# Decoder trunk on one core: forms of x tile by tile, its norm after the first gated steps, early gated tiles and weights, x tiles at multiples of 512 bytes

## The chip, the core and the metric

The kernel runs on one core of a Trainium2 chip. TensorE (PE) multiplies, VectorE (DVE) and ScalarE (ACT) prepare operands and empty PSUM, GpSimd (POOL) adds and issues accumulating DMAs, SyncE (SP) issues all other DMAs. The metric is the device time of one execution in microseconds, as the median of several runs.

## The reference

One decoder layer on 512 tokens with width 2048, in float32:

```python
h = rmsnorm(x, attn_norm)
aq, ak, av, bq, bk, bv, cq, ck, cv = split(h @ w_in)
mix = concat(rmsnorm(window_attention(aq, ak, av)), rmsnorm(stick_breaking(bq, bk, bv)),
             rmsnorm(dilated_attention(cq, ck, cv)))
x = x + mix @ w_out
h = rmsnorm(x, ffn_norm)
u = causal_dwconv(h @ w_up, conv_w, conv_b)      # width 3; w_up is 2048 x 11264
gate, up = split(u)
x = x + (silu(gate) * up) @ w_down               # w_down is 5632 x 2048
```

## The kernel before

Everything is held transposed, as tiles of 128 features by 512 tokens. A float32 product is made of three matmuls of rounded parts (`mm3`): high by high, high by low, low by high. Weights come through the three buffers `wr` in 512 KB pieces (list `stream`, `load_next`); `split` makes the parts `wh` (ACT copy) and `wl` (DVE subtraction) of each half.

The program has four stages on PE.

1. The input projection and attention. The normalised input stands in 32 tiles `x` (high and low of 16 k-tiles) of the pool `xp`, the first pool from the right end of the memory. These tiles are the moving operand of 2400 matmuls of 512 columns, with attention matmuls between them. As the built program places them, each `x` tile begins 480 bytes past a multiple of 512; the other tiles that long runs of matmuls read (`mc`, `th`, `tl`, `g`) begin at multiples of 512, because the pool `tp` has a tile `end` of 480 bytes at its right end.
2. The second half of the output projection: 16 products of 24 matmuls that read the tiles `mc`. Each result goes through `projected(m)` (line 963): DVE multiplies by the row norm `rg` and adds the first half, reloaded from `xab_dram` into one of three buffers `xn`; ACT scales it to `xb`; SP stores it to `xm_dram` and reloads `xn` for m + 3 into the buffer that this store reads; for every second m, `forms` makes the seven sums of halves of two tiles, rounded into `TH` and the remainders into `TL`; `sumsq` squares on ACT (`tq`) and adds on POOL into `gacc`. Behind the last tile `row_rstd` multiplies a matrix of ones by `gacc` on PE (tile `c`), and a short chain on ACT, POOL and DVE gives the rows `r2` and `nr2`.
3. The up-projection: 44 units u of seven steps (a11, p, q, a12, v, r, a22), s = 7u + j; each step is 24 matmuls of 256 columns with `TH` and `TL`. `cast(s + 3)` on ACT and `rest(s + 3)` on DVE make a step's weight parts `hi` and `lo`, three steps ahead. The weights p and v are sums of two blocks: SP loads one, POOL issues a DMA that adds the other. q and r are sums made on DVE (`add_raw`). `after(s)` takes results out of PSUM, applies r2, the convolution and the gate, and stores the gated tile to `g_dram`.
4. The down-projection: gated tiles are reloaded (`gates`: load, ACT copy, DVE subtraction) and multiplied by `w_down`, six sums at a time in chunks of eight tiles, then ten further products.

Between stages 2 and 3, and 3 and 4, `clock.drain()` issues everything that is queued, the `c` product among it, before the next stage's matmuls. The order on each engine is written at build time: tasks wait on a modelled clock (`Clock`) and their instructions are placed when that clock reaches them; on the chip each engine's queue then runs in that order, and an instruction that waits holds up all behind it. SP's queue too.

## Time and profile before

| what | us |
|---|---|
| median of 3 runs (lowest, highest) | 2207.19 (2206.53, 2208.12) |
| the profiled execution, its own time | 2207.63 |
| its span, first to last instruction | 2205.8 |
| PE busy in the span | 2163.0 (98%) |
| DVE busy, ACT busy | 1453.4 (66%), 1148.5 (52%) |
| stage 2, starts of the first and last matmul that read `mc` | 709.18, 799.75 |
| stage 3, starts of its first and last matmul | 817.73, 1706.37 |

The page's busy time of PE counts overlapping matmuls, so it is not PE at its peak; the distance from one matmul's start to the next is read from the timeline or from long runs in the chain of waits. Waits are read by stage.

### The profile page before, as it was taken

The page shows a single profiled execution, that of the slowest core. Times are in us where ns is not written, and L with a number is a line of the kernel's source. Part 1 is how long each engine was busy: PE and PEld are TensorE (multiplying, and loading weights), DVE is VectorE, ACT ScalarE, POOL GpSimd, SP SyncE. Part 2 cuts the span into 40 slices and gives each one's busy share as a digit, 9 for nine tenths or more (in the row PEclk, how much of TensorE's full clock was granted, in tenths as well). Part 3 has the DMA queues.
Part 4 walks back from the last instruction along what each step waited for, and adds up shares of the span by engine and source line. Part 5 has one row for each costly group of instructions (what it writes and reads, how often), then busy time and mean ns, then how long its engine had stood idle before and what let it go on. Part 6 is the DMA issues. An engine that isn't in the chain of part 4 may idle for free.

```text
span 2205.8 us, 34567 instructions
## 1 busy us (share of the span) xinstructions
PE 2163.0 (98%) x13236; PEld 1935.8 (88%) x13236; DVE 1453.4 (66%) x2229; ACT 1148.5 (52%) x2020; POOL 181.5 (8%) x241
## 2 busy tenths in 40 slices
PE   8999999999999969999999999999999899999999
PEld 6888888888888859999999999999999688888887
DVE  7677777767755687888888888788877434322222
ACT  6778667776663555555555555555554333222221
POOL 4000100110000120000000000000000000000000
PEclk9999999999999989999999999999999899999999
DMA  6322343334657557777777777777773554433332
GB/s 199 99 91 82 105 143 126 109 122 131 211 181 236 160 163 199 189 200 188 204 194 196 195 197 192 200 200 196 193 198 107 201 168 143 158 115 115 116 123 73
DMA packets 124013, 353.82 MB, mean 160 GB/s; under 512 B 14328, under 2 KB 17784, under 8 KB 123848
## 3 DMA queue, kind: packets, MB, share of 16 engines
q1 hardware_dynamic: 111176, 305.47, 41.7%
q0 software_dynamic: 12672, 46.14, 12.9%
q8 instruction: 104, 1.70, 0.3%
q14 instruction: 61, 0.50, 0.1%
HBM read 312.18 MB, written 32.57 MB: 156 GB/s over the span
## 4 chain that ended last, share of the span: by engine, by line
PE 94%; DMA 3%; DVE 1%; issue 1%; ACT 0%; SPq 0%; POOL 0%; DVEq 0%; POOLq 0%; ACTq 0%
PE s L51 50%; PE pj L51 39%; PE po L51 3%; PE c L51 2%; DMA xm_dram<-xn 1%; DMA wr<-in_w_out_dram 1%; DVE wl L51 0%; DVE tl L51 0%; DMA xn<-xab_dram 0%; DMA wr<-in_w_in_dram 0%; SPq L129 0%; DMA g<-g_dram 0%; DMA wr<-in_w_up_dram 0%; DMA st<-in_xT_dram 0%; POOL gacc L51 0%
## 5 line engine op out<-in xcount | busy, mean ns | idle before, releaser
L51 PE MATMUL s<-th,hi 128*128 128x256 f32 x2464 | 698.6, 284 | 0.0
L51 PE MATMUL s<-tl,hi 128*128 128x256 f32 x2464 | 697.7, 283 | 0.0
L51 PE MATMUL s<-th,lo 128*128 128x256 f32 x2464 | 697.7, 283 | 0.0
L51 DVE TENSOR_TENSOR wl<-wr,wh 128x512 fp32r<-128x512 f32 (+2 forms) x430 | 298.0, 698 | 342.2 <-ACT wh L51 340.5
L51 ACT CAST wh<-wr 128x512 fp32r<-128x512 f32 (+2 forms) x430 | 256.3, 598 | 486.4 <-PE pj L51 310.0
L51 PE MATMUL pj<-x,wh 128*128 128x512 f32 x1504 | 479.2, 400 | 0.0
L51 PEld LDWEIGHTS s<-th,hi 128*128 128x128 f32 x2464 | 473.6, 192 | 0.5 <-issue 0.5
L51 PEld LDWEIGHTS s<-tl,hi 128*128 128x128 f32 x2464 | 473.6, 192 | 0.5 <-issue 0.5
L51 PEld LDWEIGHTS s<-th,lo 128*128 128x128 f32 x2464 | 473.5, 192 | 0.0
L51 PEld LDWEIGHTS pj<-x,wh 128*128 128x128 f32 x1504 | 271.4, 188 | 55.7 <-issue 2.7
L51 PE MATMUL pj<-x,wl 128*128 128x512 f32 x752 | 297.1, 395 | 0.0
L51 PE MATMUL pj<-g,wh 128*128 128x512 f32 x880 | 271.0, 389 | 0.0
L51 PEld LDWEIGHTS pj<-g,wh 128*128 128x128 f32 x880 | 165.2, 188 | 34.5
L51 DVE TENSOR_TENSOR lo<-sm,hi 128x1024 fp32r<-128x1024 f32 x88 | 107.9, 1226 | 103.8 <-ACT hi L51 103.8
L51 PE MATMUL pj<-g,wl 128*128 128x512 f32 x440 | 171.2, 389 | 0.0
L51 PEld LDWEIGHTS pj<-x,wl 128*128 128x128 f32 x752 | 141.2, 188 | 33.9
L51 ACT CAST hi<-sm 128x1024 fp32r<-128x1024 f32 x88 | 92.3, 1049 | 139.7 <-DVE sm L51 139.7
L51 DVE TENSOR_TENSOR lo<-ld,hi 128x1024 fp32r<-128x1024 f32 x111 | 137.0, 1234 | 28.9 <-ACT hi L51 28.9
L51 DVE TENSOR_TENSOR lo<-wr,hi 128x1024 fp32r<-128x1024 f32 x109 | 133.1, 1221 | 28.2 <-ACT hi L51 28.2
L51 ACT CAST hi<-ld 128x1024 fp32r<-128x1024 f32 x111 | 116.5, 1050 | 21.7 <-PE s L51 21.7
L51 ACT CAST hi<-wr 128x1024 fp32r<-128x1024 f32 x109 | 114.4, 1050 | 22.2 <-PE s L51 20.7
L51 PE MATMUL s<-g,wh 128*128 128x512 f32 x352 | 110.7, 396 | 13.5 <-ACT g L51 13.3
(168 smaller groups left out, 2716.6 us busy)
## 6 DMA issues: line engine op xcount, KB each, us to landing
ld<-in_w_up_dram SPq DMA_DIRECT2D x111, 512.0 KB, 4.5
wr<-in_w_up_dram SPq DMA_DIRECT2D x109, 512.0 KB, 4.6
wr<-in_w_down_dram SPq DMA_DIRECT2D x80, 512.0 KB, 3.5
wr<-in_w_in_dram SPq DMA_DIRECT2D x78, 512.0 KB, 3.6
ld<-in_w_up_dram POOLq DMA_DIRECT2D x45, 512.0 KB, 5.6
wr<-in_w_up_dram POOLq DMA_DIRECT2D x43, 512.0 KB, 5.6
wr<-in_w_out_dram SPq DMA_DIRECT2D x32, 512.0 KB, 4.3
g_dram<-wl SPq DMA_DIRECT2D x44, 256.0 KB, 2.6
```

The source lines that it names most:

```text
L51: res = issue(out, *args, **kwargs)
```

## The change

Stage 1: a new first pool `ep` at the right end holds the 480 byte tile `end`, so that `xp` and its `x` tiles begin at multiples of 512. Nothing else moves there: but for that one memset, the instructions of every engine keep their order up to the end of this stage.

Stage 2 to 3: `forms` becomes `even_forms`, run for the even tile of a pair (the forms 0 and 3), and `odd_forms` for the odd one. `xn` has four buffers, `xb` three. The weights of steps 0 and 1 come as two more pieces of `stream`, split in halves like `w_out`; q of the first unit is summed early. There is no drain: the 48 matmuls of steps 0 and 1 follow the last product directly, step 2 is placed when the last odd forms are, the `c` product comes between the steps 3 and 4, and r2 is wanted in `after(6)`.

Stage 3 to 4: the gated tiles 0 to 4 are brought in during unit 41 into buffers of `xn`, `xb` and `tq`; the first three pieces of `w_down` are fetched and split as if they were steps of a unit 44; the first three sums run over tiles 0 to 4 at once, then over 5 to 7, with the last `after` steps between. There is no drain here either.

```diff
+        ep = ctx.enter_context(tc.tile_pool(name="ep", bufs=1, side="right"))
...
+        stream += ["a11", "p"]
...
+                if isinstance(stream[i], str):
+                    arrival = fetch(0, stream[i])
+                    raws[i] = got[0, stream[i]], arrival
+                else:
+                    piece = wp.tile([128, stream[i].shape[1]], F32, name="wr", bufs=3)
+                    raws[i] = piece, load(piece, stream[i])
...
+        vector.memset(ep.tile([128, 120], F32, name="end"), 0.0)
...
+                    ready["xab", m] = True
...
+        tx = ctx.enter_context(tc.tile_pool(name="tx", bufs=1, side="right", reuse_waits="tile"))
         tp = tctx.enter_context(tc.tile_pool(name="tp", bufs=1, side="right", reuse_waits="tile"))
         tr = tctx.enter_context(tc.tile_pool(name="tr", bufs=1, side="right", reuse_waits="tile"))
+        cv = tx.tile([128, SM_N - SM_CONV + 32], F32, name="conv")
...
-        vector.memset(tp.tile([128, 120], F32, name="end"), 0.0)
...
-            t = tr.tile([128, S], F32, name="xn", bufs=3)
+            t = tx.tile([128, S], F32, name="xn", bufs=4)
...
+        def low(j, t, a, b):
+            vector.tensor_sub(TL[j][:, a * HS:b * HS], t, TH[j][:, a * HS:b * HS].bitcast(F32))
+        def even_forms(j):
+            a = xb[2 * j]
+            while j > 1 and ("odd", j - 2) not in ready:
+                yield 0.1
+            f = quarters[j] = tr.tile([128, 4 * HS], F32, name="sm", bufs=2)
+            scalar.copy(TH[j][:, :HS], a[:, :HS])
+            vector.tensor_sub(f[:, :HS], a[:, :HS], a[:, HS:])
+            yield
+            scalar.copy(TH[j][:, 3 * HS:4 * HS], f[:, :HS])
+            low(j, a[:, :HS], 0, 1)
+            yield
+            low(j, f[:, :HS], 3, 4)
+            ready["even", j] = True
+        def odd_forms(j):
...
+            vector.scalar_tensor_tensor(q[2], b[:, HS:], -1.0, q[0], op0=ALU.mult, op1=ALU.subtract)
+            yield
+            scalar.copy(TH[j][:, 5 * HS:6 * HS], q[2])
+            scalar.copy(TH[j][:, HS:3 * HS], b)
             vector.tensor_sub(q[1], b[:, HS:], a[:, HS:])
-            scalar.copy(TH[j][:, HS:3 * HS], b)
-            vector.scalar_tensor_tensor(q[2], b[:, HS:], -1.0, q[0], op0=ALU.mult, op1=ALU.subtract)
             vector.scalar_tensor_tensor(q[3], q[2], -1.0, b[:, :HS], op0=ALU.mult, op1=ALU.subtract)
+            low(j, q[2], 5, 6)
...
+            scalar.copy(TH[j][:, 4 * HS:5 * HS], q[1])
+            scalar.copy(TH[j][:, 6 * HS:], q[3])
+            low(j, b, 1, 3)
...
+            low(j, q[1], 4, 5)
+            low(j, q[3], 6, 7)
+            ready["odd", j] = True
...
+                yield from (odd_forms if m % 2 else even_forms)(m // 2)
...
+            if u == NFF:
+                return load(t, w_down[0][DOWN.index(name)])
...
+                first = u == 0 and name == "q"
+                t = got[u, name] = place() if first else tr.tile([128, 1024], F32, name="sm", bufs=2)
+                vector.tensor_add(t, got[u, a], got[u, b])
...
+        def first_sum():
+            while len(raws) < len(stream):
+                yield 0.1
+            yield max(raws[len(stream) - 1][1] - clock.now(), 0.01)
+            fetch(0, "a12")
+            add_raw(0, "q", "p", "a11")
...
-            fetch(0, "v")
-            fetch(0, "a22")
-            for x in range(3):
-                if x == 2:
-                    add_raw(0, "q", "p", "a11")
-                cast(x)
-                yield
-                rest(x)
-                yield
-        spawn(ahead())
-        clock.drain()
...
+        while (0, "q") not in got:
+            idle()
+        def second():
+            cast(2)
+            yield
+            rest(2)
+        spawn(second())
+        fetch(0, "v")
+        fetch(0, "a22")
...
+            if s == 2:
+                add_raw(u, "r", "q", "a12")
...
-        for j in range(5):
-            after(7 * NFF + j)
-        clock.drain()
...
-        GS = {f: [gq.tile([128, S], F32R, name=f"g{x}_{f}") for x in range(2)]
-              for f in [*range(36, NFF), *range(36)]}
...
+            while s == 2 and ("odd", 7) not in ready or s == 6 and "r2" not in ready:
+                idle()
+            after(s)
+            if u == NFF - 3 and j < 5:
+                names = [f"tq{i}" if i < 3 else "xb" if i < 6 else "xn" for i in (2 * j, 2 * j + 1)]
+                GS[j] = [tx.tile([128, S], F32R, name=x, bufs={"xn": 4, "xb": 3}.get(x, 1)) for x in names]
+                spawn(gates(j))
...
+            pieces = operands(s)
+            per = 8 // len(pieces)
+            for k in range(8):
+                while ("even" if form in (0, 3) else "odd", k) not in ready:
+                    idle()
+                hi, lo = pieces[k // per]
...
-        for x in range(3):
-            split_next()
...
-        sums = [ps.tile([128, S], F32, name=x, bufs=1) for x in ("s0", "s1", "s2", "s3", "po0", "c0")]
-        for f in range(8):
-            spawn(gates(f))
+        sums = [ps.tile([128, S], F32, name=x, bufs=1) for x in ("s0", "s2", "po0", "c0", "s1", "s3")]
+        for f in range(5, NFF - 8):
+            GS[f] = [gq.tile([128, S], F32R, name=f"g{x}_{f}") for x in range(2)]
+            if f < 8:
+                spawn(gates(f))
...
+        def first_part(m, ks):
+            hi, lo = ops[7 * NFF + m][0]
+            for k in ks:
+                while ("g", k) not in ready:
+                    idle()
+                mm3(sums[m], hi, lo, k, ready["g", k], k == 0, False)
+                clock.run()
+        for m in range(3):
+            first_part(m, range(5))
+            after(7 * NFF + m)
+            clock.run()
+        for m in range(3):
+            first_part(m, range(5, 8))
+            if m < 2:
+                after(7 * NFF + 3 + m)
+            clock.run()
+            if m == 1:
+                for x in range(3):
+                    split_next()
+        for i, f in enumerate(range(NFF - 8, NFF)):
+            t = wq.tile([128, 1024], F32R, name="hi" if i < 4 else "lo", bufs=4)
+            GS[f] = [t[:, :S], t[:, S:]]
```

PE at the end of stage 2. Before, from the last row of the output projection; `c` is the product for the norm, `th` and `tl` the forms, `hi` and `lo` weight parts:

```order
L51 MATMUL pj0_8158<-mc_7278,wl_8121 128x512
L51 MATMUL c0_8247<-gacc_83,cst_78 128x512
L51 MATMUL s0_8258<-th0_7394,hi_8211 128x256
L51 MATMUL s0_8258<-tl0_7402,hi_8211 128x256
L51 MATMUL s0_8258<-th0_7394,lo_8212 128x256
```

And now, the same place:

```order
L51 MATMUL pj0_8211<-mc_7283,wl_8161 128x512
L51 MATMUL s0_8262<-th0_7404,wh_8181 128x256
L51 MATMUL s0_8262<-tl0_7412,wh_8181 128x256
L51 MATMUL s0_8262<-th0_7404,wl_8182 128x256
L51 MATMUL s0_8262<-th1_7405,wh_8181 128x256
```

The `c` product has gone from between the two stages; it stands 96 matmuls later.

DVE at the same place, now, from the multiplication that takes the last product out of PSUM (`tq2<-pj0`; `wl_8280` is the low part of p's second half, `lo_8277` that of q, `lo_8270` that of a12, `tl7` the remainders of the last pair):

```order
L51 TENSOR_TENSOR tq2_8250<-pj0_8211,r1_83 128x512
L51 TENSOR_TENSOR xn_8141<-tq2_8250,xn_8141 128x512
L51 TENSOR_TENSOR lo_8270<-ld_8201,hi_8269 128x1024
L51 TENSOR_TENSOR sm_8150<-xb_8195,xb_8138 128x256
L51 SCALAR_TENSOR_TENSOR sm_8150<-sm_8150,xb_8195 128x256
L51 TENSOR_TENSOR tl6_7418<-sm_8150,th6_7410 128x256
L51 TENSOR_TENSOR sm_8290<-xb_8247 128x256
L51 TENSOR_TENSOR lo_8277<-wr_8203,hi_8276 128x1024
L51 TENSOR_TENSOR wl_8280<-ld_8117,wh_8279 128x512
L51 TENSOR_TENSOR tl6_7418<-xb_8195,th6_7410 128x512
L51 TENSOR_TENSOR tl7_7419<-xb_8247,th7_7411 128x256
```

The remainder that step 0 reads last stands eleventh in that row, behind parts of q, p and a12; before, all of `tl7` was written before DVE read `c`.

POOL, before, with the three last additions for the norm behind the accumulating DMA of v:

```order
L51 TENSOR_TENSOR gacc_83<-gacc_83,tq2_8150 128x512
L1007 DMA wr_8206<-in_w_up_dram 128x1024
L51 TENSOR_TENSOR gacc_83<-gacc_83,tq1_8185 128x512
L51 TENSOR_TENSOR gacc_83<-gacc_83,tq0_8215 128x512
L51 TENSOR_TENSOR gacc_83<-gacc_83,tq1_8238 128x512
```

And now, with two DMAs ahead of them, v of unit 0 (`wr`) and p of unit 1 (`ld`):

```order
L51 TENSOR_TENSOR gacc_86<-gacc_86,tq0_8206 128x512
L1044 DMA wr_8257<-in_w_up_dram 128x1024
L1044 DMA ld_8266<-in_w_up_dram 128x1024
L51 TENSOR_TENSOR gacc_86<-gacc_86,tq1_8317 128x512
L51 TENSOR_TENSOR gacc_86<-gacc_86,tq0_8323 128x512
L51 TENSOR_TENSOR gacc_86<-gacc_86,tq2_8371 128x512
```

The additions now stand behind a second transfer as well.

## Rows read from the trace of the kernel before

**Rows 1.** The page: span, busy time of PE, and its clock in 40 slices.

```profile
span 2205.8 us, 34567 instructions
PE 2163.0 (98%) x13236; PEld 1935.8 (88%) x13236; DVE 1453.4 (66%) x2229; ACT 1148.5 (52%) x2020; POOL 181.5 (8%) x241
PEclk9999999999999989999999999999999899999999
```

**Rows 2.** Waits of PE: who waited for whom, us in total, times, longest.

```profile
PE c L51 <- POOL gacc L51: 16.5, 1, 16.5
PE s L51 <- ACT g L51: 13.3, 1, 13.3
```

**Rows 3.** The chain of waits, long runs of matmuls: start, us, what, count.

```profile
46.11 11.89 PE pj L51 x51
...
818.71 887.95 PE s L51 x7392
...
1902.86 299.21 PE pj L51 x1320
```

**Rows 4.** Timeline of PE at the end of stage 1: start, us, instructions.

```profile
707.78 0.63 PE L51 MATMUL pj<-x,wh 128*128 128x512 f32 x2
...
708.48 0.63 PE L51 MATMUL pj<-x,wh 128*128 128x512 f32 x2
...
709.18 0.62 PE L51 MATMUL pj<-mc,wh 128*128 128x512 f32 x2
...
709.87 0.61 PE L51 MATMUL pj<-mc,wh 128*128 128x512 f32 x2
```

**Rows 5.** Groups of PE by form: count, busy us and mean ns, idle before.

```profile
L51 PE MATMUL pj<-x,wh 128*128 128x512 f32 x1504 | 479.2, 400 | 0.0
L51 PE MATMUL pj<-x,wl 128*128 128x512 f32 x752 | 297.1, 395 | 0.0
```

**Rows 6.** Waits of SP from 709 to 800, and of DVE from 709 to 820.

```profile
SPq L129 <- DMA xm_dram<-xn: 48.6, 12, 5.3
...
DVE xn L51 <- DMA xn<-xab_dram: 16.9, 11, 3.0
```

**Rows 7.** Timeline and chain of waits between stages 2 and 3: PE, POOL and one DMA.

```profile
799.75 0.39 PE L51 MATMUL pj<-mc,wl 128*128 128x512 f32 x1
...
804.19 5.18 DMA wr<-in_w_up_dram
...
810.00 0.88 POOL L1007 DMA_DIRECT2D wr<-in_w_up_dram  x1 [11.31 <-DVE sm L51]
810.60 5.98 POOL L51 TENSOR_TENSOR gacc<-gacc,tq 128x512 f32<-128x512 f32 x3
816.64 2.07 PE L51 MATMUL c<-gacc,cst 128*128 128x512 f32 x2 [16.50 <-POOL gacc L51]
...
830.97 0.28 PE L51 MATMUL s<-th,hi 128*128 128x256 f32 x1
```

**Rows 8.** Durations: two groups of DVE, 780 to 818; two groups and a DMA of the page.

```profile
L51 DVE TENSOR_TENSOR tq<-pj,r 128x512 f32<-128x512 f32 x5 | 3.4, 682 | 0.0
L51 DVE TENSOR_TENSOR tl<-xb,th 128x256 fp32r<-128x256 f32 x4 | 1.7, 415 | 0.0
...
L51 DVE TENSOR_TENSOR lo<-wr,hi 128x1024 fp32r<-128x1024 f32 x109 | 133.1, 1221 | 28.2 <-ACT hi L51 28.2
...
L51 ACT CAST hi<-wr 128x1024 fp32r<-128x1024 f32 x109 | 114.4, 1050 | 22.2 <-PE s L51 20.7
...
wr<-in_w_up_dram POOLq DMA_DIRECT2D x43, 512.0 KB, 5.6
```

**Rows 9.** Chain of waits and timeline between stages 3 and 4.

```profile
1699.93 6.73 PE s L51 x56
...
1719.97 1.52 PE L51 MATMUL s<-g,wh 128*128 128x512 f32 x2 [13.33 <-ACT g L51]
...
1745.10 5.44 PE po L51 x24
```

More of the change, by code (lines that the diff above doesn't have):

```diff
@@ L226, in load_next @@
             if i < len(stream):
-                raw = wp.tile([128, stream[i].shape[1]], F32, name="wr", bufs=3)
-                raws[i] = raw, load(raw, stream[i])
+                if isinstance(stream[i], str):
[4 more added lines that the diff above has]
+                    raws[i] = piece, load(piece, stream[i])
                 at["load"] = i + 1
@@ L925, in program @@
                 m += 1
-            while "rg" not in ready or any(("mix", i) not in ready for i in MIX_ORDER[8:]):
+            while ("rg" not in ready or any(("mix", i) not in ready for i in MIX_ORDER[8:])
+                   or any(("xab", i) not in ready for i in range(KT))):
                 idle()
@@ L965, in task @@
                 t = xs2[m]
-                sq = yield from take(tr, "tq")
+                sq = yield from take(tx, "tq")
                 vector.tensor_mul(sq, pt, rg)
@@ L971, in task @@
                 yield
-                b = tr.tile([128, S], F32, name="xb", bufs=4)
+                while m > 2 and ("odd", (m - 3) // 2) not in ready:
+                    yield 0.1
+                b = tx.tile([128, S], F32, name="xb", bufs=3)
                 xb.append(b)
                 scalar.activation(b, t, AF.Copy, scale=sm[:, SM_FG + m:SM_FG + m + 1])
+                done = scalar.free
                 load(xm_dram[m], t)
@@ L999, in fetch @@
         def fetch(u, name):
-            if u >= NFF:
+            if u > NFF or u == NFF and name not in DOWN:
                 return
-            t = raw[u, name] = place()
+            t = got[u, name] = place()
+            if u == NFF:
+                return load(t, w_down[0][DOWN.index(name)])
             first, second = {"a11": ((0, 0), None), "a12": ((0, 1), None), "a22": ((1, 1), None),
                              "p": ((1, 0), (1, 1)), "v": ((0, 0), (1, 0))}[name]
-            load(t, w_up[u, first[0], first[1]])
+            arrival = load(t, w_up[u, first[0], first[1]])
@@ L1108, in after, with operands @@
                 load(g_dram[v], c)
-        for s in range(7 * NFF):
-            u, j = divmod(s, 7)
-            if j == 0:
-                psy[u] = ps.tile([128, S], F32, name=f"s{u % 2}", bufs=1)
-                psz[u] = ps.tile([128, S], F32, name=f"s{2 + u % 2}", bufs=1)
-                for name in ("a11", "p", "a12"):
-                    fetch(u + 1, name)
-            if j == 3:
-                for name in ("v", "a22"):
-                    fetch(u + 1, name)
-            after(s)
-            name, form, chain = STEPS[j]
-            to = {"y": psy[u][:, A], "x": psz[u][:, A], "z": psz[u][:, B]}[chain]
-            hi, lo = ops.pop(s)
-            for k in range(8):
-                c, t = slice(k * 128, (k + 1) * 128), slice(form * HS, (form + 1) * HS)
-                tensor.matmul(to, hi[:, c], TH[k][:, t], start=j < 2 and k == 0, stop=False, skip_group_check=True)
-                tensor.matmul(to, hi[:, c], TL[k][:, t], start=False, stop=False, skip_group_check=True)
-                tensor.matmul(to, lo[:, c], TH[k][:, t], start=False, stop=k == 7, skip_group_check=True)
-            clock.run()
-        for j in range(5):
-            after(7 * NFF + j)
-        clock.drain()
-        wctx.close()
-        tctx.close()
-        gq = ctx.enter_context(tc.tile_pool(name="gq", bufs=1, reuse_waits="tile"))
-        GS = {f: [gq.tile([128, S], F32R, name=f"g{x}_{f}") for x in range(2)]
-              for f in [*range(36, NFF), *range(36)]}
+        def operands(s):
+            if s < 2:
+                ops[s] = []
+                for _ in range(2):
+                    while at["use"] not in parts:
+                        idle()
+                    ops[s].append(parts.pop(at["use"]))
+                    at["use"] += 1
+                    split_next()
+            return ops.pop(s)
+        GS = {}
         def gates(f):
@@ L1177, in program @@
                             spawn(gates(f))
[L1178 removed]
+                if c or m > 2:
+                    accumulate(sums[m], [("g", f) for f in range(c0, c0 + n)], range(n), None, c == 0,
+                               c == len(chunks) - 1)
                 if c == len(chunks) - 1:
```

104 lines of the change are left out of this document (60 added, 44 removed).

## The prediction

> **What bounds the kernel now.** I read the page first, then the waits of PE, then long runs of matmuls, and last the two places where PE stops.
>
> PE is busy 98% of a span of 2205.8 us and its clock stands at full speed in nearly all of the 40 slices [rows 1]. So two things can give time: fewer nanoseconds per matmul, and the places where PE stands still. The waits of PE name two: 16.5 us before the norm's product `c`, ended by POOL's `gacc`, and 13.3 us before the first product with a gated tile, ended by ACT [rows 2]. They are where the program drains, between stages 2 and 3, and 3 and 4.
>
> For the nanoseconds I divide runs by their counts [rows 3]. 51 matmuls with `x` take 11.89 us, 233.1 ns each. 1320 with `g`, also 512 columns, take 299.21 us, 226.7 ns each. The 7392 of 256 columns with `th` and `tl` take 120.1 ns each. The timeline shows the step from one rate to the other [rows 4]: groups of three start at 707.78, 708.48 and 709.18 while `x` is read (0.70 us) and at 709.18 and 709.87 once `mc` is (0.69, the first of them at the seam). Weights, shape and PSUM buffers are of the same kind on both sides; the moving operand has changed.
>
> The forecast is made against the profiled execution, 2207.63 us (span 2205.8 and 1.8 around it); the median of the runs is 0.4 us lower.
>
> **Part 1, the place of x.** One memset is added at the start and no other instruction moves. Of the tiles that long runs read, only `x` begins off a multiple of 512 bytes, and only `x` is slow. `g` tiles fill nearly the whole memory, so it isn't the region; DVE and ACT work beside `mc` as they do beside `x`, so it isn't their traffic. If the offset is the cause, each of the 1504 + 752 matmuls into `pj` [rows 5] gains 233.1 - 226.7 = 6.46 ns, 14.6 us in all. The 144 others that read `x` lie in the first 40 us, which wait for transfers; I count them at nothing (at most 0.9). What hides the gain would be attention work that comes late: PE hardly waits for it now, and the other engines follow PE's pace, so I take 14 us (12 to 15.5).
>
> [...]
>
> **Part 2, inside stage 2.** 384 matmuls read `mc`; from the first start, 709.18, to the last, 799.75, are 90.57 us [rows 4, 7], and 383 steps of 226.7 ns are 86.81. So 3.8 us are lost in small waits. SP explains them: 12 times, 48.6 us together, it waits until a store of `xn` has landed before it may reload that buffer [rows 6], and the next piece of `w_out` stands behind that in its queue. DVE waits 16.9 us for the same reloads [rows 6]. With four buffers the reload goes where the store before last read, some 5.4 us older than now, and such a transfer lands in about 4 to 5. Against that, the split forms add DVE instructions: per pair of tiles the 1024-wide remainder (1.22) becomes four of 0.415 [rows 8], 0.4 us in 10.9, and DVE loses its wait. I take 2.5 us (0 to 3.8).
>
> **Part 3, between stages 2 and 3.** Call the end of the last product zero. Before, that is 799.75 + 0.23 = 799.98, and the matmul at 830.97 [rows 7] is the 97th of stage 3, the first of step 4: 30.99 us. After, step 4 also follows steps 0 to 3 and `c`; the question is when.
>
> Steps of 24 matmuls take 2.88 us. Step 0 can start at zero, as its weights and the forms of pairs 0 to 6 are made during the last product; its last three matmuls want `tl7`. DVE's queue from zero has, in the order printed: two of 0.68, one of 1.22, four of 0.42, one of 1.22, two of 0.68, and `tl7`, 0.42 [rows 8]: 7.3 us, all of it behind the last product. So PE does 2.5 us of step 0, waits 4.8, and ends it at 7.5. Step 1 ends at 10.4; its late half of p (`wl`, at 6.1) and `tl7` (at 8.5) are there.
>
> Step 2 wants the odd forms of pair 7, and these stand on ACT and DVE behind the parts of v. Named in order: SP loads the first block of v when DVE has written the sum of tile 14, about -2.7; such a load took 5.18 [rows 7], so 2.5; POOL adds the second block, 5.6 to landing [rows 8], so about 8.7 with the issue; ACT's copy 1.05, DVE's remainder 1.22 and the first odd form 0.42 [rows 8] make 11.4; ACT copies it (an estimate of 0.6 from 1.05 for four times the width) while DVE makes two more forms, and the remainder follows, 3 x 0.415: 12.7. Step 2's last matmuls come at 10.4 + 2.5 = 12.9, so they just do not wait, and step 3 ends at 16.2.
>
> `c` comes next and wants `gacc`. The three last additions stand on POOL behind the DMAs of v and of p of unit 1. p's first block may be loaded when DVE has split the old one in that buffer (6.1); 5.2 more make 11.3, the issue 0.9 [rows 7], and the additions 3.9 to 6.0 (5.98 as measured [rows 7], where DVE worked beside them; I guess two thirds of that at best): 16.2 to 18.2. I take the later, as DVE is as busy there. `c` takes 1.1 (two parts, 2.07 [rows 7], of which the second overlaps), so step 4 starts at 19.3. That saves 30.99 - 19.3 = 11.7 us; I take 11.5. The best case is no wait before `c` (17.3, gain 13.7); if a load takes 5 us more and PE's clock falls in the pauses, as one slice of the row of its clock shows for the gap of before [rows 1], 24 (gain 7).
>
> After `c` the norm's chain (ACT, POOL, DVE) is wanted in `after(6)`, two steps or 5.8 us behind step 4's start. It stands on POOL behind the DMA of v of unit 1. What waits for it is DVE, and matmuls read what DVE makes there three steps later, so 8.6 us of PE's work covers it; without that cover the wait for one more load, 5.2, is lost, which the late end of 24 holds.
>
> **Part 4, between stages 3 and 4.** Before, the last step ends at 1699.93 + 6.73 = 1706.66, and 96 matmuls later, at 1745.10, the fifth sum starts [rows 9]. The work is 96 x 226.7 ns = 21.76 us, so 16.7 are lost: the wait of 13.3 and a slow start (the first two matmuls last 1.52 us [rows 9]).
>
> After, the first 45 matmuls (10.2 us) read tiles 0 to 4, brought in 40 us earlier, and weights split on the old pattern of three steps ahead. Tiles 5 to 7 land into buffers free some microseconds before the end of the stage; a load of 5.2, a copy of about 0.6 and a subtraction of 0.68 put them at about 6 us, an estimate from rows 7 and 8; they are wanted at 10.2. The next weights (27 matmuls on, at 16.3) are loaded before the stage ends. The last `after` steps run beside this. I take 16 us (12 to 16.7). In unit 41 DVE has five more subtractions of 0.68, 3.4 us in the 20 of a unit, and ACT as many copies; PE waits for neither in that stage.
>
> **Sum.** 14 + 2.5 + 11.5 + 16 = 44 us: 2207.6 - 44 = 2163.6, and with the median 0.4 lower, 2163. The ends of the four parts are 31 (12 + 0 + 7 + 12) and 49.7 (15.5 + 3.8 + 13.7 + 16.7): 2158 to 2176.
>
> **Rivals.** A: the distance of matmuls doesn't depend on where `x` begins. For it: attention matmuls on other tiles in stage 1 are mixed with these and not clearly quicker. Against: the step in rows 4, at once and with the tile. Then 14 us are missing: 2177. Chance 0.08.
>
> B: the wait between stages 2 and 3 is only renamed. PE does steps 0 and 1 and then waits for v behind ACT's and DVE's queues, or for `gacc` behind two DMAs. For it: POOL's additions stand behind one transfer more than before. It decides if p's block lands 8 us later than I put it; step 4 then starts at about 27 and the gain is 4: 2170.5. Chance 0.11.
>
> C: the first sums wait for tiles 5 to 7 or weights as before, because their loads stand behind a store of SP that is late; 8 us lost again: 2171. Chance 0.05.
>
> D, the slower one: what sets the rate is the place of a tile and not its offset in 512. All of `th` and `tl` move down by 22016 bytes, and 7392 matmuls read them. If they then cost 6.46 ns more each, that is 47.8 us, against 30 from the other parts: 2207 - 30 + 48 = 2225. It decides from 4 ns on. Against: `g` has one rate all over the memory. Chance 0.02.
>
> E: gains in all places are lost again behind, as DVE falls behind in stage 2 and stays the bound into stage 3: within 4 us of before. Against: DVE is busy 66% [rows 1]. Chance 0.02.
>
> **How the numbers follow.** The forecast has 0.72, and its own range is 2158 to 2170. The range to hold 8 in 10 takes in B and C and half of A: 2157 to 2177. A difference under 0.2% (4.4 us) is about what these measurements cannot tell from none. Faster by more: forecast, A, B and C, 0.96. Same: E, 0.02. Slower: D, 0.02.
>
> **What the profile will show.** Right: runs with `x` at 226.7 ns each; stage 2 within 1 us of 87 for its 384 matmuls, without SP's waits for the stores of `xn`; PE's pause inside step 0 near 5 us ended by DVE `tl`, one of about 2 us before `c` ended by POOL; no pause and no slow matmul before the first tiles of stage 4; `th` at 120 ns. Wrong: `x` still at 233; one pause over 8 us before step 2 or `c`; a pause at stage 4's start or 10 us behind it.

## The result, and the profile after

After takes 2170.55 us (median of 4 runs, 2170.25 to 2171.75), before beside it 2207.07 (2206.53 to 2208.12): a ratio of 0.9835, 95% interval 0.9818 to 0.9852. The profiled executions are 2170.64 and 2207.63, so 37.0 us were gained where 44 were forecast. The page of after, the lines that answer to [rows 1]:

```profile
span 2168.9 us, 34584 instructions
PE 2150.6 (99%) x13236; PEld 1935.5 (89%) x13236; DVE 1460.3 (67%) x2252; ACT 1150.1 (53%) x2043; POOL 180.4 (8%) x241
PEclk9999999999999999999999999999999999999999
```

The waits of PE after (who waited for whom, us in total, times, longest). The two of [rows 2] are gone; the largest that is left lies at the start of the program, the other two between stages 2 and 3:

```profile
PE s L51 <- ACT wh L51: 5.4, 1, 5.4
PE s L51 <- DVE tl L51: 4.6, 2, 3.3
PE s L51 <- ACT th L51: 1.8, 1, 1.8
```

Stretches of PE in after, in us from the span's start: length, PE busy (instructions), granted clock, share of the DMA engines, GB/s. First stage 2 from its first start to its last; then step 0, step 1, and steps 2 and 3 with `c`; then the first 96 matmuls of stage 4:

```profile
700.43:787.24 86.81, 86.81 (x385) 1.00 0.62 193
787.47:796.25 8.78, 3.64 (x25) 0.91 0.75 223
796.25:801.37 5.12, 5.12 (x25) 0.50 0.81 234
801.37:810.58 9.21, 7.54 (x52) 0.99 0.38 67
1686.18:1707.97 21.79, 21.79 (x98) 1.00 0.49 179
```

(A count includes matmuls that only end in the stretch.) With [rows 4, 7, 9] these give the gain by parts. The first `mc` comes at 700.43, before at 709.18. Stage 2 takes 86.81 us, before 90.57. From the end of the last product (787.24 + 0.23 = 787.47) to step 4 (810.58) are 23.1 us, before 30.99. The 96 matmuls take 21.79 us and begin 0.12 behind the last `th`.

| part | forecast (range), us | measured, us |
|---|---|---|
| 1, x | 14 (12 to 15.5) | 8.8 |
| 2, inside stage 2 | 2.5 (0 to 3.8) | 3.8 |
| 3, between stages 2 and 3 | 11.5 (7 to 13.7) | 7.9 |
| 4, between stages 3 and 4 | 16 (12 to 16.7) | 16.6 |
| sum | 44 (31 to 49.7) | 37.0 (the parts, rounded, 37.1) |

Two questions follow: why `x` gave 8.8, and what holds step 4 back.

### The profile page after: what moved, and what is told of

It reads as the page before. It is cut to its first block, busy times and chain, and to the rows that moved or that the text cites. A ratio compares the mean times of both kernels' runs of the same rounds, so it can differ in the third digit from the quotient of the medians.

```text
span 2168.9 us, 34584 instructions
## 1 busy us (share of the span) xinstructions
PE 2150.6 (99%) x13236; PEld 1935.5 (89%) x13236; DVE 1460.3 (67%) x2252; ACT 1150.1 (53%) x2043; POOL 180.4 (8%) x241
## 4 chain that ended last, share of the span: by engine, by line
PE 97%; DMA 2%; DVE 1%; issue 0%; SPq 0%; ACT 0%; POOLq 0%; DVEq 0%
PE s L51 51%; PE pj L51 41%; PE po L51 3%; PE c L51 2%; DMA ld<-in_w_up_dram 1%; DMA wr<-in_w_up_dram 0%; SPq L129 0%; DVE wl L51 0%; DVE sm L51 0%; DMA st<-in_xT_dram 0%; DMA wr<-in_w_in_dram 0%; DMA cst<-in_consts_dram 0%; DVE tl L51 0%; DVE sq L51 0%; DVE lo L51 0%
## 5 line engine op out<-in xcount | busy, mean ns | idle before, releaser
L51 PE MATMUL pj<-x,wh 128*128 128x512 f32 x1504 | 473.5, 396 | 0.0
L51 PE MATMUL pj<-g,wh 128*128 128x512 f32 x620 | 190.7, 389 | 0.0
L51 PEld LDWEIGHTS pj<-g,wh 128*128 128x128 f32 x620 | 116.4, 188 | 24.1
L51 PE MATMUL pj<-g,wl 128*128 128x512 f32 x310 | 120.6, 389 | 0.0
L51 DVE CUSTOM_DVE_ANT_0 sc<-s,strip 128x128 f32<-128x128 f32 (+3 forms) x96 | 43.6, 455 | 74.6 <-PE s L51 72.8
```

Of the source, the lines that this page charges most:

```text
L51: res = issue(out, *args, **kwargs)
```

## Experiments on the place of an operand

**align**: part 1 alone.

```diff
--- before
+++ align
+        ep = ctx.enter_context(tc.tile_pool(name="ep", bufs=1, side="right"))
...
+        vector.memset(ep.tile([128, 120], F32, name="end"), 0.0)
...
-        vector.memset(tp.tile([128, 120], F32, name="end"), 0.0)
```

> The kernel before, with nothing but the 480 byte tile moved ahead of the x tiles, so that these begin at multiples of 512 bytes. Theory 1 (settling): in the trace of after, a run of matmuls with x goes at about 232 ns for its first matmuls behind other work and only then at 226.7; the runs of stage 1 are short, so the gain is what after shows up to its first matmul with mc, 8.75 us: 2198.8 us, between 2198 and 2200. Theory 2 (the prediction's): each of the 2256 matmuls gains 6.46 ns and after lost 5 us of that elsewhere in stage 1: 2193.5 us. Rival A (the place does not matter, the gain of after came from something else): 2207 us.

Measured: 2199.44 us, before beside it 2206.43, ratio 0.9965 (0.9952 to 0.9978). That is the time of theory 1. Its two groups of matmuls with `x` have word for word the rows that after has (count, then busy us and mean ns; before, [rows 5]: 479.2 and 297.1):

```profile
L51 PE MATMUL pj<-x,wh 128*128 128x512 f32 x1504 | 473.5, 396 | 0.0
L51 PE MATMUL pj<-x,wl 128*128 128x512 f32 x752 | 294.3, 391 | 0.0
```

In its trace the first `mc` comes at 700.77, 8.4 us earlier than before. In the drain between stages 2 and 3 it loses 1.7 of these again (32.7 us from the last product to step 4, before 31.0), with `c` waiting 17.5 us for `gacc` (16.5 before). So part 1 is worth some 8.5 us, not 14, also without the other parts.

**rate**: rows of matmuls and nothing else; `run(o, n)` issues n of them with the operand at offset o, and the last line has the weights at 96 (24 words).

```diff
+        offsets = (0, 32, 64, 96, 128, 256, 480)
...
+        for o in offsets:
+            run(o, 96)
+        for _ in range(4):
+            run(96, 24, wl)
+            run(0, 24)
...
+        run(0, 96, wl, S, 24)
```

> Leaves the whole computation out: only rows of 128x512 matmuls with one operand whose first byte stands 0, 32, 64, 96, 128, 256 or 480 past a multiple of 512, then 24 matmuls at offset 96 or 480 and 24 at 0 in turn, 24 with 128 columns and 24 with 512 in turn, rows of 256 and of 128 columns, and weights at offset 96. Theory 1: 0 goes at 226.7 ns each and 480 at 233, and 0 behind 96, 480 or 128 columns starts at about 232 and settles at 226.7 after 5 to 11 matmuls. If the unit is 64 bytes, 64, 128 and 256 go at 226.7 and 32 and 96 at 233; if it is 512 bytes, all but 0 go at 233. Theory 2: 0 goes at 226.7 from its first matmul on, whatever ran before. Rival A: all rows at one rate.

Four stretches of it: the whole row at 0, the whole row at 32, and of a row at 0 behind one at 96 the first eight matmuls and eight of the last nine (columns as above, with PEld, DVE, ACT and POOL between PE and the clock):

```profile
30.29:52.05 21.76, 21.76 (x97) 18.02 (x96) 0.00 (x0) 0.00 (x0) 0.00 (x0) 1.00 0.00 0
52.05:74.46 22.41, 22.41 (x98) 17.99 (x96) 0.00 (x0) 0.00 (x0) 0.00 (x0) 1.00 0.00 1
191.04:192.88 1.84, 1.84 (x9) 1.50 (x8) 0.00 (x0) 0.00 (x0) 0.00 (x0) 1.00 0.00 0
194.70:196.52 1.82, 1.82 (x9) 1.50 (x8) 0.00 (x0) 0.00 (x0) 0.00 (x0) 1.00 0.00 0
```

21.76 / 96 = 226.7 ns and 22.41 / 96 = 233.4. The third row is 1.84 / 8 = 230 and the fourth 1.82 / 8 = 227.5 by rounded ends; start by start, the matmuls at 0 behind a row at 96 stand 229, 234, 235, 225, 230, 236, 229, 232, 231 ns apart, and from then on 226 or 227 without exception. Behind 24 at 480 the good rate comes after 5 matmuls, behind 128 columns after 10, behind three at 96 after 3 to 6. So the good place gives the good rate only once a run has settled. Stage 1 has 226 runs of `x`, with a median of 6 matmuls; 174 of them, with 987 of the 2256 matmuls, are no longer than 12. The traces of before and after show the loss start by start: over the 2030 steps from one matmul of such a run to the next the gain is 8.0 us, where 6.46 ns each would be 13.1. On the mean the first three steps of a run gained at most 0.9 ns, those from the tenth on 6 or more. That is where the missing 5 us of part 1 are. The same is seen in one place of after, where a run of `x` behind four small matmuls begins at 304.20: nine matmuls in 2.08 us (231 ns each), then seven in 1.59 (227).

```profile
304.53:306.61 2.08, 2.08 (x11) 1.00 0.80 234
306.61:308.20 1.59, 1.59 (x8) 1.00 0.59 224
```

The other rows of rate were not foreseen by any theory: 512 columns go at 226.7 also at 256, at 228.9 at 64 and at 233.3 at 32, 96, 128 and 480; weights at 96 with the operand at 0 give 234.3; 256 columns go at 120.0 at 0, but at 117.8 at 32 and 64; and 128 columns at 111.7 everywhere.

**grid** asks whether operand (`o`) and weights (`start`) count each for itself or by their distance; S is 512 columns, HS 256.

```diff
+        for start in (0, 32, 64, 128, 256):
+            for cols in (S, HS):
+                for o in range(0, 512, 32):
+                    run(o, 36, cols, start)
```

> Leaves the whole computation out: rows of 36 matmuls, the moving operand's first byte at 0, 32, ... 480 past a multiple of 512, with 512 and with 256 columns, for weights whose first byte stands at 0, 32, 64, 128 and 256. In the rows of rate, with weights at 0, 512 columns went at 226.7 ns each at 0 and 256, 228.9 at 64 and 233.3 at 32, 96, 128 and 480, and 256 columns at 120.0 at 0, 96 and 256 but 117.8 at 32 and 64; weights at 96 with the operand at 0 gave 234.3. Theory 1 (two reads that meet): the rate depends on the distance between weights and operand, so weights at 32 with the operand at 32 go at 226.7 again, and the row of rates is shifted by the weights' offset. Theory 2 (each for itself): with weights off 0 or 256 no operand of 512 columns goes below 229, and the rates of 256 columns do not shift.

Eighteen settled matmuls each. With 512 columns: weights 0 and operand 0, 0 and 32, 32 and 0, 32 and 32. With 256 columns: 0 and 0, 0 and 192, 32 and 192, 32 and 224, 64 and 0:

```profile
34.76:38.84 4.08, 4.08 (x20) 3.38 (x19) 0.00 (x0) 0.00 (x0) 0.00 (x0) 1.00 0.00 0
43.02:47.22 4.20, 4.20 (x20) 3.38 (x19) 0.00 (x0) 0.00 (x0) 0.00 (x0) 1.00 0.00 0
236.51:240.71 4.20, 4.20 (x19) 3.38 (x18) 0.00 (x0) 0.00 (x0) 0.00 (x0) 1.00 0.00 0
244.81:248.90 4.09, 4.09 (x20) 3.38 (x19) 0.00 (x0) 0.00 (x0) 0.00 (x0) 1.00 0.00 0
166.87:169.03 2.16, 2.16 (x20) 2.16 (x19) 0.00 (x0) 0.00 (x0) 0.00 (x0) 1.00 0.00 0
192.42:194.46 2.04, 2.04 (x20) 2.04 (x19) 0.00 (x0) 0.00 (x0) 0.00 (x0) 1.00 0.00 0
394.14:396.25 2.11, 2.11 (x21) 2.11 (x19) 0.00 (x0) 0.00 (x0) 0.00 (x0) 1.00 0.00 0
398.33:400.37 2.04, 2.04 (x20) 2.04 (x19) 0.00 (x0) 0.00 (x0) 0.00 (x0) 1.00 0.00 0
570.16:572.28 2.12, 2.12 (x20) 2.12 (x19) 0.00 (x0) 0.00 (x0) 0.00 (x0) 1.00 0.00 0
```

Theory 1 holds in 158 of the 160 rows, with another unit: what counts is the place of the operand minus that of the weights, in bytes modulo 256, called the distance from here on. With 512 columns a distance of 0 gives 226.7 ns, 64 gives 228.9, the rest 233.3 to 234.5. With 256 columns: 0 and 96 give 120.0, 32 and 64 give 117.8, 128 gives 118.4 to 118.9, 160 gives 117.4, 224 gives 118.5, and **192 gives 113.3** in nine rows of ten, wherever both stand. The two rows that differ are the last one above, weights 64 and operand 0, which is a distance of 192 and ran at 117.8, and weights 128 and operand 32, a distance of 160, at 118.7. So one distance can have two rates; fine and phase come back to this. In before, `x` stood at a distance of 224 from its weights; `th` and `tl` stand at 0 in both kernels, which for 256 columns is a poor place.

So with nothing else running, the rate in these rows depends on where operand and weights stand to each other: 113.3 to 120.0 ns with 256 columns, 226.7 to 234.5 with 512. What makes it so, no run here shows.

**th192** uses it: `th` and `tl` moved by 192 bytes, no instruction moved.

```diff
--- after
+++ th192
-        vector.memset(ep.tile([128, 120], F32, name="end"), 0.0)
+        vector.memset(ep.tile([128, 56], F32, name="end"), 0.0)
...
-        cv = tx.tile([128, SM_N - SM_CONV + 32], F32, name="conv")
+        cv = tx.tile([128, SM_N - SM_CONV + 48], F32, name="conv")
```

> After, with the tiles th and tl moved by 192 bytes, so that they begin 192 past a multiple of 256 (x, mc and g stay at multiples of 256, all weights at multiples of 512). Theory (distance of operand and weights modulo 256): the rows of grid give 113.3 ns for 256 columns at a distance of 192 in place of 120.0 at 0; 7392 matmuls gain 6.7 ns, 49.5 us; as their three matmuls per k alternate between two operands and two weights, some may settle elsewhere: 2121 to 2127 us. Rival (other engines): a step falls from 2.88 to 2.72 us, and the weights' chain of transfer, ACT and DVE, or the transfers, bound it: 2130 to 2165 us. Rival (rows of one kind only): in the mixed order of the kernel the rate is 118 to 120 as before: 2160 to 2171 us.

Measured: of four executions three took 2121.95 to 2124.20 us, a ratio to before of 0.9617 (0.9601 to 0.9632), and one 2155.92. **both** adds the order of qvc2 (below):

> The kernel of qvc2 with th and tl at 192 past a multiple of 256 as in th192. Theory: the two gains add, 3.1 us from the order between stages 2 and 3 and 49.5 from the distance of operand and weights: 2118 to 2124 us. Rival (other engines bound stage 3): as in th192, less 3 us.

Measured: one execution at 2118.75, three between 2150.24 and 2150.93; beside before's 2207.41 that is 0.960 and 0.974. The same stretch of stage 3, of after, of th192 and of both (in the profile of both, an execution of 2150.74), in this order:

```profile
830.00:1640.00 810.00, 810.00 (x6753) 1.00 0.73 198
```

```profile
830.00:1640.00 810.00, 810.00 (x7139) 1.00 0.76 208
```

```profile
830.00:1640.00 810.00, 810.00 (x6882) 1.00 0.75 202
```

The clock is granted in full in all three; 810 us over the counts are 119.9, 113.5 and 117.7 ns. So DVE, ACT and the transfers follow a step that is 5% shorter. The fast execution of both was not profiled; it is 31.7 us shorter than the median of the four, which is 4.5 ns over some 7100 matmuls, the difference of the two rates. Start by start, in its profile, both runs at 113.3 ns from 822.9 to 840.8, then has one step of 207 ns, and runs at 117.8 from there to the end of the stage; th192 has such short stops at 823.84 and 843.35 and is back at 113.3 within six and two matmuls.

**fine** and **phase** look at what chooses between the rates.

```diff
+        for cols in (S, HS):
+            for o in range(0, 256, 8):
+                run(o, 36, cols, 0)
```

> Leaves the whole computation out: rows of 36 matmuls with 512 and with 256 columns, the moving operand's first byte at 0, 8, 16, ... 248, weights at 0. Theory (lines of 32 bytes): the rates of grid hold for 32 bytes each, nothing below 226.7 and 113.3. Rival (any step of the offset counts): new rates between them, perhaps lower ones near 192.

The rival holds. Steps of 8 bytes count: with 256 columns 112 also gives 113.3 and 16 gives 116.7, with 120 beside them; with 512 columns nothing but 0 reaches 226.7, and 120 gives 240.0.

phase puts other work ahead of each row, and turns at another distance into it.

```diff
+        for o in range(0, 256, 32):
+            for n in range(1, 7):
+                run(96, n, 384, 0)
+                run(o, 36, HS, 0)
+        for o in range(0, 256, 32):
+            for n in (1, 4):
+                run(96, n, 384, 0)
+                for _ in range(8):
+                    run(192, 21, HS, 0)
+                    run(o, 3, HS, 0)
```

> Leaves the whole computation out: rows of 36 matmuls of 256 columns at eight distances from the weights, each row behind 1 to 6 matmuls of 384 columns or 1 to 12 of 512 at another distance; and rows of 21 at distance 192 and 3 at another one in turn. th192 ran at 113.3 ns per matmul to the end of the stage in its profile, the kernel of both, with the same distance, at 117.8, into which it fell at a short stop at 840 us. Theory (two steady states at 192): among the rows at 192 some settle at 113.3 and some at 117.8, by what ran before them; the other distances have states of their own. Rival (one state, and both was slow for another reason, such as its clock): all rows at 192 settle at 113.3. Open: whether three matmuls at another distance in every 24 bring the rate back to 113.3 each time.

Rows at 192 behind 3 and 6 matmuls of 384 columns (eighteen matmuls each), and the first two of eight rounds of 21 at 192 and 3 at 32 behind 4 of them:

```profile
218.91:221.03 2.12, 2.12 (x21) 2.12 (x19) 0.00 (x0) 0.00 (x0) 0.00 (x0) 1.00 0.03 8
234.24:236.28 2.04, 2.04 (x21) 2.04 (x19) 0.00 (x0) 0.00 (x0) 0.00 (x0) 1.00 0.03 8
333.49:336.32 2.83, 2.83 (x26) 2.83 (x25) 0.00 (x0) 0.00 (x0) 0.00 (x0) 1.00 0.00 0
336.32:339.07 2.75, 2.75 (x26) 2.75 (x25) 0.00 (x0) 0.00 (x0) 0.00 (x0) 1.00 0.00 0
```

At 192 there are two steady rates, 113.3 (behind 1, 2 and 6) and 117.8 (behind 3, 4 and 5); which one a row takes depends on what ran before. Behind matmuls of 512 columns at another distance it was 117.8 behind one and 113.3 behind 2 to 12. Some other distances have more than one rate too (32: 116.7 and 117.8; 160: 117.3 to 118.8). The first round with 32 runs at 117.8 (2.83 us); its three matmuls at 32 bring the next rounds to 113.3 and keep them there (2.75 each, of which the turn costs 0.03). Turns at 0, 64, 96, 128 and 160 keep 113.3 as well; the rounds with 224 began at 117.8 and stayed there.

**kick** puts such a turn into each unit of both.

```diff
--- both
+++ kick
-        TH = [tp.tile([128, 7 * HS], F32R, name=f"th{j}") for j in range(8)]
-        TL = [tp.tile([128, 7 * HS], F32R, name=f"tl{j}") for j in range(8)]
+        TH = [tp.tile([128, (7 - (j == 7)) * HS], F32R, name=f"th{j}") for j in range(8)]
+        TL = [tp.tile([128, (7 - (j == 7)) * HS], F32R, name=f"tl{j}") for j in range(8)]
+        tk = tp.tile([128, 24 + S], F32R, name="tk")
+
+        def part(T, j, a, b):
+            if (j, a) == (7, 6):
+                return tk[:, 24:24 + HS] if T is TH else tk[:, 24 + HS:]
+            return T[j][:, a * HS:b * HS]
...
```

> The kernel of both, with the parts of the last form of pair 7 (three matmuls of the last step of each unit, 3 in 168) in a tile of their own at distance 32, the rest of th and tl at 192. In the rows of phase, 21 matmuls at 192 and 3 at 32 in turn came back to 113.3 ns each time, from 117.8 too, and the 24 took 114.7 each on the mean, 35 ns more for one such turn. Theory (a turn resets the state): no execution stays at 117.8; every one takes 2119 to 2124 us, 44 turns costing 1.5 us against the fast run of both (2118.75). Rival (once in 168 is too seldom, or the turn ends elsewhere in the order of the kernel): times fall into two groups again, near 2120 and near 2150 us, or all lie near 2150.

Measured: 2120.61 us, all five executions between 2119.76 and 2120.89, ratio to before 0.9606 (0.9592 to 0.9619). The stretch of stage 3:

```profile
830.00:1640.00 810.00, 810.00 (x7115) 1.00 0.74 208
```

113.8 ns on the mean. Start by start its trace shows the turn at work. At 840.0 it has the kind of stop at which both fell to 117.8 for the rest of the stage, and it falls too; the next turn comes at 853.8, and behind it 113.3 is back. 72 matmuls on each side of that turn:

```profile
842.86:851.34 8.48, 8.48 (x74) 1.00 0.98 231
855.54:863.70 8.16, 8.16 (x74) 1.00 0.70 180
```

This is the fastest kernel here that stays so in every execution: 86.6 us under before, 50 under after.

## Experiments on the place between stages 2 and 3

The chain of waits of after from the first transfer of p to the last odd forms (start, us, what):

```profile
771.37 6.67 DMA ld<-in_w_up_dram
...
778.68 5.66 DMA ld<-in_w_up_dram
...
784.37 0.04 DVE wr L51
...
788.45 4.43 DMA wr<-in_w_up_dram
...
793.50 5.52 DMA wr<-in_w_up_dram
...
799.05 1.05 ACT hi L51
...
800.13 1.23 DVE lo L51
801.35 3.66 DVE sm L51 x2
```

p lands at 784.3; DVE adds q (`wr`), which had waited for it, and everything of the last two tiles stands behind. SP's load of v follows at 788.45, the transfer by which POOL adds v's second block lands at 799.0, ACT and DVE make v's parts, and behind them DVE makes the odd forms of the last pair, two operations of 0.42 in 3.66. Three moves were tried.

**q_late**: q's addition behind the even forms of the last pair.

```diff
             fetch(0, "a12")
+            while ("even", 7) not in ready:
+                yield 0.1
             add_raw(0, "q", "p", "a11")
```

> After, with the first q (a DVE addition of 1024 columns that waits for the second transfer of p) placed behind the even forms of the last pair instead of ahead of them. Theory (DVE's queue): the first pause stands behind that addition, the remainders of q and a12 and two other parts; taking q and these two behind tl7 brings tl7 some 5 us forward, the two pauses of step 0 (1.8 and 3.3 us) fall under 1 us together, step 1 runs at 120 ns per matmul instead of 213 (2.2 us back), and the parts of v start some 2 us earlier; the first matmul of step 4 comes 18 to 20 us after the last product instead of 23.1: 2166 to 2168 us. Rival (transfers): the pause is set by transfers and by ACT, and what is taken out of DVE's queue ahead of tl7 comes back ahead of step 2: 2169.5 to 2171 us.

Measured: 2177.42 us, 6.9 more than after; both theories missed. Timeline of PE and of DVE in q_late (start, us, operation, idle time before and what ended it):

```profile
792.66 0.38 PE L51 MATMUL s<-tl,wh 128*128 128x256 f32 x1 [1.90 <-DVE tl L51]
...
806.30 0.58 PE L51 MATMUL s<-th,wl 128*128 128x256 f32 x1 [9.40 <-DVE wl L51]
```

```profile
803.29 2.36 DVE L51 TENSOR_TENSOR lo<-wr,hi 128x1024 fp32r<-128x1024 f32 x2 [7.07 <-ACT hi L51]
805.56 0.69 DVE L51 TENSOR_TENSOR wl<-ld,wh 128x512 fp32r<-128x512 f32 x1
```

The two pauses of step 0 became one of 1.90 (the theory wanted under 1), but the remainder of v now stood ahead of that of q and of p's second half in DVE's order: DVE waited 7.07 us for v, and step 1 waited 9.40 for `wl` behind it. A part that step 4 reads held up step 1.

**vc**: the odd forms ahead of v's parts, and `c` between steps 5 and 6.

```diff
-            while s == 2 and ("odd", 7) not in ready or s == 6 and "r2" not in ready:
+            while s == 1 and ("odd", 7) not in ready or s == 6 and "r2" not in ready:
                 idle()
+            if s == 5:
+                ready["late"] = True
...
+                    while "late" not in ready:
+                        yield 0.1
                     yield from row_rstd(tx, acc, D, r2, nr2)
```

> After, with the odd forms of the last pair placed ahead of the parts of v (they stood behind), and the norm's product c two steps later, between steps 5 and 6. Theory (v ahead of the forms): the pauses of step 0 and the slow step 1 stay, the 1.66 and 0.67 us before and in step 2 go, and c no longer waits; step 4 comes about 20 us after the last product instead of 23.1, c costs 0.9 later: 2167.5 to 2168.5 us. Rival (contention): DVE runs at a third of its speed while POOL adds (2.31 us for an operation that takes 0.42), whatever its order, so step 2 still waits 1 to 2 us: 2169.5 to 2170.5 us.

Measured: 2168.58 us, ratio to before 0.9826 (0.9811 to 0.984), as the theory said. Step 4 starts 19.66 us after the last product in place of 23.1, of which 1.0 is `c`, now paid behind it; PE has no wait left in step 2, and the rival is refuted. The pauses of step 0 (2.26 and 3.34) and the slow step 1 stay.

**qvc2**: both moves (the lines of vc are in it too), and v's first block loaded early.

```diff
             fetch(0, "a12")
+            t = got[0, "v"] = place()
+            load(t, w_up[0, 0, 0])
+            while ("even", 7) not in ready:
+                yield 0.1
...
-        fetch(0, "v")
+        nc.gpsimd.dma_start(got[0, "v"], w_up[0, 1, 0], accum_op=ALU.add)
```

> After, with three moves at once: the first q behind the even forms of the last pair, the odd forms of that pair ahead of v's parts, with v's first block loaded some 7 us earlier, and c between steps 5 and 6. Theory (queues): in q_late q, its remainder and the second half of p stood behind v's parts, which waited 7 us on a transfer; here nothing that steps 0 to 3 read stands behind v. tl7 is there 5.3 us after the last product (as in q_late, 793.6 less 788.3) instead of 8.2, the last odd remainder at about 12, and step 4 starts 17 to 19 us after the last product instead of 23.1 (and about 20.5 in vc), c costs 0.9 later: 2165.5 to 2167.5 us. Rival (DVE is full): DVE has no idle time from the sum of tile 14 on, so what is taken from ahead of step 0 is missing ahead of steps 1 and 2: 2168 to 2169 us, as vc.

Measured: 2167.43 us, ratio 0.9819 (0.9803 to 0.9836), at the theory's slow end. Step 4 starts at 19.41, hardly earlier than in vc. PE's stops in steps 0 and 1:

```profile
791.67 0.38 PE L51 MATMUL s<-tl,wh 128*128 128x256 f32 x1 [1.56 <-DVE tl L51]
...
795.41 0.39 PE L51 MATMUL s<-th,wh 128*128 128x256 f32 x1 [1.81 <-ACT wh L51]
797.02 0.58 PE L51 MATMUL s<-th,wl 128*128 128x256 f32 x1 [1.11 <-DVE wl L51]
```

Step 1 starts 4.1 us earlier than in after, but it now waits itself, and from 797.4 to 802.9 its matmuls and those of step 2 stand 213 ns apart, with the clock granted at 0.50: the slow stretch has moved, not gone. DVE has work without a gap from 784 to 799; the rival (DVE is full) has the larger share.

**dve** asks why DVE's operations are long there. In after, the timeline of POOL and of DVE at the end of stage 2:

```profile
779.43 1.60 POOL L51 TENSOR_TENSOR gacc<-gacc,tq 128x512 f32<-128x512 f32 x1
781.77 3.07 POOL L51 TENSOR_TENSOR gacc<-gacc,tq 128x512 f32<-128x512 f32 x2 [0.74 <-ACT tq L51]
```

```profile
779.39 1.92 DVE L51 TENSOR_TENSOR tl<-xb,th 128x256 fp32r<-128x256 f32 x1
...
781.91 1.78 DVE L51 TENSOR_TENSOR wl<-ld,wh 128x512 fp32r<-128x512 f32 x1
784.37 1.55 DVE L51 TENSOR_TENSOR wr<-ld 128x1024 f32<-128x1024 f32 x1 [0.68 <-DMA ld<-in_w_up_dram]
```

The usual times of the three DVE operations are 0.42, 0.69 and 1.22 us. The first two took 2.6 us more, but behind them DVE still stood 0.68 for p: in after that loss is covered by the wait for p, and only the 0.33 of the third is not. In kick, where q's addition stands further back, DVE has no such wait (its chain of waits shows DVE without a gap from 779.2 to 797.4), and the loss counts.

```diff
--- kick
+++ dve
-            gpsimd.tensor_add(acc, acc, sq)
+            (vector if pool is tx else gpsimd).tensor_add(acc, acc, sq)
...
```

> The kernel of kick with the additions of the squares for the norm in stage 2 made by DVE (0.69 us each for 512 columns) in place of POOL. Theory (POOL slows DVE): in the trace of after, while POOL makes its last three additions of stage 2 (779.4 to 784.8 us), DVE operations of 0.42, 0.69 and 1.22 us take 1.92, 1.78 and 1.55, 2.9 us more than elsewhere, so DVE is 2 to 3 us late with the last tiles; with the additions on DVE each operation has its usual time, DVE pays 0.6 per addition instead, and step 1 starts 1 to 2 us earlier than in kick (4.7 us after the last product), step 4 at 16 to 17.5 instead of 18.1: 2118.5 to 2120 us. Rival (those operations wait for something else): they stay long, DVE has 0.6 us per tile more to do, and step 4 comes later: 2121 to 2123 us.

Measured: 2135.19 us, 14.6 more than kick, so the total missed. But the durations answer the question. DVE in stage 2 (701 to 787) in dve:

```profile
L51 DVE TENSOR_TENSOR wl<-wr,wh 128x512 fp32r<-128x512 f32 x29 | 19.8, 684 | 2.8 <-ACT wh L51 2.7
...
L51 DVE TENSOR_TENSOR tl<-sm,th 128x256 fp32r<-128x256 f32 x21 | 8.2, 418 | 0.1
```

The second group has 418 ns each, in after 503 and in kick 590; the first 684, after 723. So POOL's additions did stretch DVE operations that ran beside them, in after one from 0.42 to 1.92 us. The total is longer because the change of the costs moved the whole order of stage 2: in dve PE's pause before `tl7` is 8.4 us, behind p, whose second block POOL adds only from 785.99 on (778.55 in kick), and behind a reload of `xn`, for which DVE stands 2.9 us. Whether the same order without POOL's additions would be faster was not measured.

## Why the prediction was right, and where it was wrong

The time lay in the wide range (2157 to 2177) and 0.6 us beyond the forecast's own (2158 to 2170), and the four places where it was to come from were the right ones. Two terms were mis-sized, parts 1 and 3. Part 1 lay outside its own bounds; the sum held because the bounds of the other parts are wide and parts 2 and 4 came out near their best.

**Part 1** failed in the step that each of the 1504 + 752 matmuls into `pj` gains 6.46 ns. That the place sets the rate is shown by align (8.4 us up to the first `mc`) and rate (226.7 ns at 0, 233.3 at 480), and rival A is refuted. But the 6.46 ns were read from the two longest runs ([rows 3]) and multiplied by matmuls of which nearly half stand in runs of at most 12, and in rate a run needed 3 to 10 matmuls to settle. The term measured 8.8 with its low end at 12. What "hides the gain" was looked for in attention work that comes late; it lay in the runs' own beginnings. The unit was wrong too: not a tile's offset in 512 but its distance from the weights modulo 256. The sentence "only `x` begins off a multiple of 512 bytes, and only `x` is slow" fitted this by luck, as all weights stand at multiples of 512. Rival D feared the move of `th` and `tl` by 22016 bytes, a multiple of 256: their rate was 119.9 ns in after and 120.1 before ([rows 3]), at a distance of 0 in both (120.0 in grid).

**Part 2** came out at its upper end: SP's waits for the stores of `xn` are 2.3 us in place of 48.6 [rows 6], and 383 steps of 226.7 ns take 86.8 us with no loss. That this is the work of the fourth buffer is read from these waits; no run has it alone.

**Part 3** gave 3.6 us less than was taken for it (step 4 at 23.1 in place of 19.3), inside its bounds. `tl7` was put at 7.3 and came at 8.2, in two pauses, the first of 1.8 ended by ACT's `th`, which the forecast did not have. These did not set step 4. What did is the chain to the odd forms, and it failed in two steps.

The first is "DVE has written the sum of tile 14, about -2.7": that sum came at 0.1, and v's load went out at 1.0. Ahead of it in DVE's queue stands q's addition, which waits for the second block of p, landed at -3.1; the forecast did not have that wait on this path. q_late, which takes the addition out of the way, brings the sum to -0.5 and no further, as three operations ahead of it took 4.2 us more than usual beside POOL's additions.

The second is the price of DVE's operations. The forecast let POOL's additions stretch beside DVE, and put DVE's at their usual time: the first two of the odd forms took 3.66 for 0.84 as POOL's additions met them again. So the remainder that step 2 wants, put at 12.7, came at 18.2, and PE waited 1.3 us for it. Step 1, behind the two pauses, ran with the clock granted at 0.50 and took 5.1 us in place of 2.9, but that only shortened this wait: vc, with the odd forms ahead of v's parts and the same slow step 1, has step 4 some 2.5 us earlier, `c` left aside. The forecast's own last link, `gacc` before `c`, did not bind: there was no wait before `c`, as step 3 ended later than the additions. Rival B's shape was there at half its size; that the time is B's 2170.5 is chance, as the larger loss lies in part 1.

**Part 4** held: the first gated tiles, the weights and the clock were all there (21.79 us for 96 matmuls at a clock of 1.00). How much of it the early tiles give and how much the early weights was not tried.

## What to carry to other kernels

Read a matmul's rate in long runs and in short ones apart, and count how many stand in which before multiplying. Where one rate stands above another with equal shapes, try the distance between the operand's and the weights' first bytes modulo 256 in a kernel of bare rows; here moving two sets of tiles by 192 bytes took 46 to 49 us off 2170, in three of four executions of th192 and, with the turn, in all of kick. When an operation is moved forward in a queue, look for what it lets pass: q_late lost 7 us because a part that step 4 wants slipped ahead of one that step 1 wants.

## What the hardware showed that was not expected

- In grid, at a granted clock of 1.00 in every stretch above, the rate of matmuls depends on the place of the operand minus that of the weights modulo 256: 113.3 to 120.0 ns for 256 columns, 226.7 to 234.5 for 512 (in fine, with steps of 8 bytes, up to 121.3 and 240.0). The best distance for 512 columns, 0 (226.7), is among the worst for 256 (120.0).
- In rate a run at 0 settled over 3 to 10 matmuls, and in phase a distance of 192 has two steady rates for 256 columns, 113.3 and 117.8 ns, at the same granted clock of 1.00; in the profile of both the rate went from 113.3 to 117.8 at a stop of one matmul (207 ns) and stayed there for nearly 7000. Three matmuls at another distance in each unit brought 113.3 back in kick, behind the turn at 853.8.
- In after, a DVE operation beside an addition of 512 columns on POOL took 1.92 us in place of 0.42; in dve, with these additions on DVE, the same kind took 418 ns each.
